# One block of a transformer on one core: the heads of an attention pair side by side in the matrix engine, and the gates' blocks between the pairs

## The chip, the cores and the metric

The kernel runs on one core of a Trainium2 chip. Five engines work there, each on a queue of its own that it takes in order: TensorE (PE, matmuls and transposes into the PSUM memory), VectorE (DVE), ScalarE (ACT), GpSimd (POOL) and SyncE (SP, which issues the loads). The metric is the device time of one execution in microseconds (us); lower is better.

## What is computed

The reference is two transformer blocks on 256 tokens of 1024 channels, in float32. The change is in the first half of the first block: a normalisation, one large projection, two attentions of 8 heads with 64 channels each, and a gated sum.

```python
h = rmsnorm(x, norm1_g)
qa, ka, va, qb, kb, vb, ga, gb = split(h @ w_in)
ya = neighbourhood_attention(qa, ka, va, rpb)        # scores + bias, window mask, softmax, @ va
qh = axial_rope(rmsnorm(qb, gqa_q_norm_g))           # rotation by row and column of the grid
kh = axial_rope(rmsnorm(kb, gqa_k_norm_g))
yb = gqa_attention(qh, kh, vb)                       # 8 query heads on 2 key/value heads
merged = sigmoid(ga) * (ya @ w_proj_a) + sigmoid(gb) * (yb @ w_proj_b)
x = x + merged @ w_out
```

Behind it come a layer of 16384 small experts (peer), and a second block with two recurrent mixers and a mixture of experts; the change leaves all of that as it is.

## The kernel before

A float32 product is done as three products of rounded parts. `split` (L65) makes the parts: ACT copies a value in rounded form (`whi`, L66), and DVE, or POOL where `eng` says so, subtracts that from the value (`wlo`, L67). `mm3` (L78) issues the three matmuls. `load_w` (L70) loads one block of weights, 128 partitions by 1024 values (512 KB), into a buffer `raw` and splits it. There are 4 `raw` buffers and 2 pairs of `whi` and `wlo`.

`block1_mix` (L143) is the first half of the first block. The normalised tokens lie transposed in `hT`. Then, in the order of the source:

- `qk_block` (L174): 8 blocks of 24 matmuls of 256 columns, queries and keys of the neighbourhood attention. In between the bias window and the mask are loaded, and POOL adds the mask to all of the bias at once (L246).
- `moving` (L179): 4 blocks of 12 matmuls of 512 columns for the values `va` (L256).
- four calls of `attention` (L197), one for each pair of heads.
- `moving` for the queries (4 blocks, `pq`) and for keys and values (2 blocks of 24 matmuls of 256 columns, `pkv`) of the second attention; then the rotation chain (L266 to L309) for both tiles of 128 tokens: squares, their sums, a reciprocal root by Newton steps (`rstd`, L92), products with the gains and the rotation's tables, all on DVE, then transposes `pqT` and `pkT` on PE and copies of them to `qT` and `kT`.
- four more calls of `attention`.
- 16 gate blocks (L316): `stationary` (L168), 24 matmuls of 256 columns each into a tile `pg`, copied by ACT into `sg`. The first 8 have their `wlo` made by POOL. At the end ACT takes four sigmoids of 4 blocks each (L321).

One call of `attention` does two heads `j`, whose queries and keys lie in partitions 0 to 63 and 64 to 127. Per head: scores `pS` (two matmuls of 64 rows, L204); in the neighbourhood attention DVE scales them and adds the bias (L211); DVE takes the negated maximum `mx`; ACT takes the exponentials with their sums (L220); DVE multiplies by the reciprocal sums (L224); PE transposes (`pT`, L228), and ACT copies the result (`PT`, L230). Then four matmuls `pY` (L235) multiply with the values of both heads, for each `j` all 128 columns of which only its own 64 are used, and `split` writes the halves of `yT`.

PSUM buffers come by tag: "mm" (4, projections and gates), "att" (2, `pS` and `pY`), "tr" (2, transposes). A scheduler that runs when the program is built sets the order of the instructions in each engine's queue: by order of the source, as far as it holds operands ready and buffers free; SP's order up to L251 is that of the source. What it fixes is final: on the chip each engine takes its queue in order.

Behind this part come the projections `pp` (L326 on), 8 blocks of 24 matmuls, which need the sigmoids and both `yT`.

## Time and profile before

| what | value |
|---|---|
| median of 3 runs | 1756.07 us (1755.73 to 1756.47) |
| the profiled execution, its own time | 1763.74 us |
| its span in the profile | 1761.9 us |
| PE busy | 1660.2 us, 94% of the span |
| DVE busy | 1133.1 us, 64% |
| ACT busy | 750.5 us, 43% |
| POOL busy | 190.5 us, 11% |
| the chain that ended last | PE 67%, DVE 18%, DMA 7%, issue 4%, ACT 3% |

Busy time is a share of the whole span; a stage has its own limit, and what an engine waits for is read from the timeline of that stage. In a timeline a row has the start, the duration, the engine, the line of the kernel, the operation and its tiles, and at the end, in brackets, how long the engine had been idle and who ended the wait. Float32 matmuls of this kernel count two records each, those of rounded parts one. PEclk is the clock that PE was granted, as a share of 2.4 GHz.

### The profile page before, as it was taken

The numbers are of one execution on the slowest core, as the hardware profiler recorded it, in microseconds if no ns is written. First come the engines' busy times: TensorE is split into PE (matmuls) and PEld (weight loads), VectorE is DVE, ScalarE is ACT, GpSimd is POOL, SyncE is SP. The second block draws the span as 40 slices with busy tenths as digits, with TensorE's granted clock in tenths as the row PEclk, the third lists the DMA queues.
The fourth block names the chain that finished last, engine by engine and source line by source line (L and its number), as shares of the span: only waits on it lengthen the run. The fifth ranks groups of instructions, "written<-read, shape, count | busy, mean of one in ns | idle before, by whom it ended". The sixth has DMA issues, their size and how long they took to land.

```text
span 1761.9 us, 29814 instructions
## 1 busy us (share of the span) xinstructions
PE 1660.2 (94%) x11419; PEld 1307.8 (74%) x11419; DVE 1133.1 (64%) x2214; ACT 750.5 (43%) x1224; POOL 190.5 (11%) x95
## 2 busy tenths in 40 slices
PE   6989999899989999999999997987989999999996
PEld 6778888899989999777788776977875444444443
DVE  5675779995989999877777767688673111111112
ACT  3547544444544444444444455655552222222222
POOL 1030001222111222000000003023020000000000
PEclk9999999999999999999999999998999999999999
DMA  6423654556545555587888754532067799999993
GB/s 232 131 84 109 214 163 158 160 158 192 155 126 162 169 171 177 172 283 265 308 283 295 261 165 144 181 118 72 13 238 282 266 392 409 409 402 409 409 409 132
DMA packets 108118, 390.91 MB, mean 222 GB/s; under 512 B 12656, under 2 KB 12944, under 8 KB 107840
## 3 DMA queue, kind: packets, MB, share of 16 engines
q1 hardware_dynamic: 106128, 384.58, 62.7%
q0 software_dynamic: 976, 2.82, 0.5%
q8 instruction: 91, 1.49, 0.3%
q10 hardware_dynamic: 864, 1.53, 0.3%
q14 instruction: 59, 0.48, 0.1%
HBM read 386.79 MB, written 2.10 MB: 221 GB/s over the span
## 4 chain that ended last, share of the span: by engine, by line
PE 67%; DVE 18%; DMA 7%; issue 4%; ACT 3%; POOL 0%; SPq 0%; DVEq 0%; ACTq 0%
PE pgu L1559 11%; PE acc L686 10%; PE py L1578 6%; PE pu L80 5%; PE pu L81 5%; PE pu L82 5%; DVE wlo L67 5%; DMA raw<-in_w_ada 4%; PE pga L1743 3%; PE py L1840 3%; PE pg L632 2%; ACT whi L66 2%; PE pmv L81 1%; PE pmv L82 1%; PE pmv L80 1%
## 5 line engine op out<-in xcount | busy, mean ns | idle before, releaser
L66 ACT ACTIVATE whi<-raw 128x1024 fp32r<-128x1024 f32 x366 | 384.5, 1054 | 307.7 <-PE pu L81 136.7
L67 DVE TENSOR_TENSOR wlo<-raw,whi 128x1024 fp32r<-128x1024 f32 x310 | 383.4, 1239 | 83.1 <-ACT whi L66 82.0
L82 PE MATMUL pu<-pxT,wlo 128*128 128x256 f32 x1024 | 289.7, 283 | 9.2 <-DVE wlo L67 6.7
L80 PE MATMUL pu<-pxT,whi 128*128 128x256 f32 x1024 | 292.3, 285 | 0.8 <-ACT whi L66 0.8
L81 PE MATMUL pu<-pxT,whi 128*128 128x256 f32 x1024 | 288.9, 282 | 0.0
L686 PE MATMUL acc<-whi,hh 128*128 128x512 f32 x1008 | 280.7, 396 | 8.5 <-ACT hh L66 5.8
L686 PEld LDWEIGHTS acc<-whi,hh 128*128 128x128 f32 x1008 | 189.1, 189 | 53.9 <-ACT hh L66 6.8
L67 POOL TENSOR_TENSOR wlo<-raw,whi 128x1024 fp32r<-128x1024 f32 x56 | 149.6, 2675 | 661.9 <-ACT whi L66 607.2
L82 PEld LDWEIGHTS pu<-pxT,wlo 128*128 128x128 f32 x1024 | 195.3, 191 | 11.1 <-DVE wlo L67 8.1
L80 PEld LDWEIGHTS pu<-pxT,whi 128*128 128x128 f32 x1024 | 195.4, 191 | 1.0 <-ACT whi L66 1.0
L81 PEld LDWEIGHTS pu<-pxT,whi 128*128 128x128 f32 x1024 | 195.4, 191 | 0.0
L1559 PE MATMUL pgu<-raw,xg 128*32 128x512 f32 (+2 forms) x1012 | 193.8, 597 | 0.0
L686 PE MATMUL acc<-wlo,hh 128*128 128x512 f32 x504 | 157.5, 393 | 2.8 <-DVE wlo L67 2.8
L66 ACT ACTIVATE hh<-H 128x256 fp32r<-128x256 f32 x126 | 52.6, 417 | 174.6 <-PE acc L686 169.9
L1559 PEld LDWEIGHTS pgu<-raw,xg 128*32 128x32 f32 (+2 forms) x1012 | 55.6, 124 | 92.3 <-issue 82.1
L686 PEld LDWEIGHTS acc<-wlo,hh 128*128 128x128 f32 x504 | 95.0, 189 | 24.3 <-DVE wlo L67 4.2
L67 DVE TENSOR_TENSOR yl<-py,yh 128x512 fp32r<-128x512 f32 x52 | 36.0, 691 | 110.7 <-ACT yh L66 110.6
L1578 PE MATMUL py<-raw,th 128*32 128x512 f32 (+2 forms) x504 | 99.9, 599 | 0.5 <-ACT th L1572 0.5
L1564 DVE SCALAR_TENSOR_TENSOR hh<-hh,sv,pgu 128x256 f32<-128x256 f32 x26 | 12.4, 478 | 124.5 <-ACT hh L1563 124.5
L771 DVE SCALAR_TENSOR_TENSOR ada<-raw,cs,ada 128x1024 f32<-128x1024 f32 x48 | 61.5, 1282 | 40.6 <-DMA raw<-in_w_ada 40.6
L1746 ACT ACTIVATE xg<-pga 128x256 f32<-128x256 f32 x104 | 40.0, 384 | 111.6 <-PE pga L1743 107.6
L1743 PEld LDWEIGHTS pga<-S,hs 128*128 128x128 f32 x416 | 54.5, 188 | 36.8 <-issue 36.1
(567 smaller groups left out, 2919.5 us busy)
## 6 DMA issues: line engine op xcount, KB each, us to landing
raw<-in_w_gu SPq DMA_DIRECT2D x186, 512.0 KB, 9.6
raw<-in_peer_u SPq DMA_DIRECT2D x128, 512.0 KB, 3.6
raw<-in_peer_v SPq DMA_DIRECT2D x128, 512.0 KB, 4.5
raw<-in_w_dn SPq DMA_DIRECT2D x90, 512.0 KB, 10.1
raw<-in_w_ada SPq DMA_DIRECT2D x48, 512.0 KB, 4.8
raw<-in_w_in_a SPq DMA_DIRECT2D x24, 512.0 KB, 3.6
raw<-in_w2a SPq DMA_DIRECT2D x17, 512.0 KB, 4.4
raw<-in_w_out SPq DMA_DIRECT2D x16, 512.0 KB, 3.6
```

The source lines that it names most:

```text
L66: e.nc.scalar.activation(hi, src, AF.Copy)
L67: (eng or e.nc.vector).tensor_sub(lo, src, hi.bitcast(F32))
L80: nc.tensor.matmul(out, lh, rh, start=first, stop=False)
L81: nc.tensor.matmul(out, lh, rl, start=False, stop=False)
L82: nc.tensor.matmul(out, ll, rh, start=False, stop=last)
L686: nc.tensor.matmul(acc[tt][n], h[l][:, s], w[r][:, n * 512:(n + 1) * 512], start=j == order[0] and i == 0, stop=j == order[-1] and i == 2)
L771: nc.vector.scalar_tensor_tensor(mod[n], w, cs[:, c:c + 1], mod[n], op0=OP.mult, op1=OP.add)
L1559: nc.tensor.matmul(pg[t], xx[:, c, t], ws[i][:, k * 512:(k + 1) * 512], start=c == 0, stop=c == NC8 - 1)
L1578: nc.tensor.matmul(py[q][t], th[:, k, t], w[i][:, q * 512:(q + 1) * 512], start=k == 0, stop=last and k == 1)
L1743: nc.tensor.matmul(p[:, :n].rearrange("p u n -> p (u n)"), hs[i][:, tt, q * P:(q + 1) * P], S[:, tt, :n].rearrange("p u n -> p (u n)"), st ...
L1746: nc.scalar.activation(xg[:, q, :n], p[:, :n], AF.Copy)
L1840: nc.tensor.matmul(acc[tt][n], St[:, tt * P:(tt + 1) * P], y[:, n * 512:(n + 1) * 512], start=first and v == 0 and w == 0, stop=v == len(u ...
```

## The change

It does five things, all in `block1_mix`.

- `attention` issues the scores of both heads first, one matmul of each head in turn, and then the softmax of the one and of the other. `pY` has four matmuls of 64 columns each, head 0 into partitions 0 to 63 and head 1 into 64 to 127 of one tile, in turn; the tile has the tag "mm" now, not "att". One `split` of 128 partitions follows in place of two of 64.
- `moving` for the second attention and the rotation chain stand ahead of the first `attention`.
- Two gate blocks follow each call of `attention`, in place of 16 behind the last.
- All `wlo` of the gates are made by DVE. The mask is added by DVE too, in four parts of 768 columns.
- The blocks of `w_in` are loaded by `wide_load` (L1407), a helper of the later layers, with 4 pairs of `whi` and `wlo`: the two old ones and two more in the pool `b1`. It takes the places of a list in turn:

```python
def load(src, whole=False, eng=None):
    raw.append(raw.pop(0))
    pool, bufs, tag = raw[-1]
    t = pool.tile([P, 1024], F32, tag=tag, name=uid(e, "raw"), bufs=bufs) if bufs else pool
    e.nc.sync.dma_start(t, src)
...
    parts.append(parts.pop(0))
    pool, bufs = parts[-1]
    hi, lo = (pool.tile([P, 1024], F32R, tag=g, name=uid(e, g), bufs=bufs) for g in ("whi", "wlo"))
    split(e, hi, lo, t, eng)
    return hi, lo
```

```diff
--- before.py
+++ after.py
@@ -164,9 +164,10 @@
 
 
     qkT = pool.tile([P, 8, T], F32, name="qkT")
+    load = wide_load(e, [(e.stage, e.raw_bufs)], [(e.stage, e.w_bufs), (pool, 2)])
 
     def stationary(blk, out, eng=None):
-        wh, wl = load_w(e, a["w_in_a"][blk], eng=eng)
+        wh, wl = load(a["w_in_a"][blk], eng=eng)
         wh, wl = (w.rearrange("p (c n) -> p c n", c=NC8) for w in (wh, wl))
         for c in range(NC8):
             mm3(e, out, wh[:, c], wl[:, c], hT[0][:, c], hT[1][:, c], c == 0, c == NC8 - 1)
@@ -180,7 +181,7 @@
 
         pt = [ps.tile([P, 512], F32, tag="mm", name=uid(e, "pmv"), bufs=e.mm_bufs) for _ in range(2)]
         for i, b in enumerate(blks):
-            wh, wl = load_w(e, a["w_in_b"][b])
+            wh, wl = load(a["w_in_b"][b])
             wh, wl = (w.rearrange("p (c n) -> p c n", c=per) for w in (wh, wl))
             for k in range(per):
                 c = i * per + k
@@ -196,12 +197,14 @@
 
     def attention(pair, q_of, k_of, v_of, bias_of, dst):
 
+
+        heads = [slice(j * 64, (j + 1) * 64) for j in range(2)]
+        pSs = [ps.tile([P, 2, T], F32, tag="att", name=uid(e, "pS"), bufs=e.att_bufs) for _ in heads]
+        for i, tt in enumerate((1, 0)):
+            for s, pS in zip(heads, pSs):
+                nc.tensor.matmul(pS[:, i], q_of(pair)[s, tt * P:(tt + 1) * P], k_of(pair)[s], start=True, stop=True)
         PT = []
-        for j in range(2):
-            s = slice(j * 64, (j + 1) * 64)
-            pS = ps.tile([P, 2, T], F32, tag="att", name=uid(e, "pS"), bufs=e.att_bufs)
-            for i, tt in enumerate((1, 0)):
-                nc.tensor.matmul(pS[:, i], q_of(pair)[s, tt * P:(tt + 1) * P], k_of(pair)[s], start=True, stop=True)
+        for j, pS in enumerate(pSs):
             S = wk.tile([P, 2, T], F32, tag="S", name=uid(e, "S"), bufs=2)
             mx = wk.tile([P, 2], F32, tag="mx", name=uid(e, "mx"), bufs=3)
             sm = wk.tile([P, 2], F32, tag="sm", name=uid(e, "sm"), bufs=3)
@@ -229,13 +232,11 @@
             pt = wk.tile([P, 2, T], F32, tag="PT", name=uid(e, "PT"), bufs=4)
             nc.scalar.activation(pt, pT, AF.Copy)
             PT.append(pt)
-        pY = ps.tile([P, 2, T], F32, tag="att", name=uid(e, "pY"), bufs=e.att_bufs)
-        for j in range(2):
-            for kc in range(2):
-                nc.tensor.matmul(pY[:, j], v_of(pair, kc), PT[j][:, kc], start=kc == 0, stop=kc == 1)
-        for j in range(2):
-            s = slice(j * 64, (j + 1) * 64)
-            split(e, dst[0][s, pair], dst[1][s, pair], pY[s, j])
+        pY = ps.tile([P, 512], F32, tag="mm", name=uid(e, "pY"), bufs=e.mm_bufs)[:, :T]
+        for kc in range(2):
+            for s, pt in zip(heads, PT):
+                nc.tensor.matmul(pY[s], v_of(pair, kc)[:, s], pt[:, kc], start=kc == 0, stop=kc == 1)
+        split(e, dst[0][:, pair], dst[1][:, pair], pY)
 
     for b in (0, 4, 1, 5):
         qk_block(b)
@@ -243,8 +244,6 @@
     nc.sync.dma_start(bias.rearrange("p a b c -> p (a b c)"), a["na_win"])
     mask = pool.tile([P, 64], F32, name="mask")
     nc.sync.dma_start(mask, a["na_mask"])
-    nc.gpsimd.tensor_tensor(bias.rearrange("p a b c -> p (a b) c"), bias.rearrange("p a b c -> p (a b) c"),
-                            mask[:, None, :].to_broadcast([P, 48, 64]), op=OP.add)
     rope = pool.tile([P, 2, 2, 64], F32, name="rope")
     nc.sync.dma_start(rope.rearrange("p a b c -> p (a b c)"), a["rope"])
     gqk = [row(e, pool, a["gqa_q_norm_g"], 64, "gq", eng=nc.sync), row(e, pool, a["gqa_k_norm_g"], 64, "gk", eng=nc.sync)]
@@ -254,11 +253,6 @@
         qk_block(b)
     for tt, p in enumerate(moving(range(0, 4), 512, 2)):
         nc.vector.tensor_copy(va[:, tt], p)
-    bv = bias.rearrange("p h v c -> p h (v c)")
-    for pair in range(4):
-        attention(pair, lambda q: qkT[:, q], lambda q: qkT[:, 4 + q],
-                  lambda q, kc: va[:, kc, q * P:(q + 1) * P], lambda h: bv[:, h], yT[0])
-
 
     pq = moving(range(4, 8), 512, 2)
     pkv = moving(range(8, 10), 256, 4)
@@ -307,16 +301,32 @@
         for k in range(2):
             nc.tensor.transpose(p[:, k], kf[:, k * P:(k + 1) * P], e.ident)
         nc.vector.tensor_copy(kT[:, :, tt * P:(tt + 1) * P], p[:, :2])
+
+    sg = keep.tile([P, 16, T], F32, name="sg")
+
+    def gate(b):
+        p = ps.tile([P, 512], F32, tag="mm", name=uid(e, "pg"), bufs=e.mm_bufs)
+        stationary(8 + b, p[:, :T])
+        nc.scalar.activation(sg[:, b], p[:, :T], AF.Copy)
+
+    bv = bias.rearrange("p h v c -> p h (v c)")
+
+    def masked(h):
+        if h % 2 == 0:
+            v = bias[:, h:h + 2].rearrange("p a b c -> p (a b) c")
+            nc.vector.tensor_tensor(v, v, mask[:, None, :].to_broadcast([P, 12, 64]), op=OP.add)
+        return bv[:, h]
+
+    for pair in range(4):
+        attention(pair, lambda q: qkT[:, q], lambda q: qkT[:, 4 + q],
+                  lambda q, kc: va[:, kc, q * P:(q + 1) * P], masked, yT[0])
+        for b in (2 * pair, 2 * pair + 1):
+            gate(b)
     for pair in range(4):
         attention(pair, lambda q: qT[:, q], lambda q: kT[:, q // 2],
                   lambda q, kc: vb[:, kc, q // 2].rearrange("p a b -> p (a b)"), None, yT[1])
-
-
-    sg = keep.tile([P, 16, T], F32, name="sg")
-    for b in range(16):
-        p = ps.tile([P, 512], F32, tag="mm", name=uid(e, "pg"), bufs=e.mm_bufs)
-        stationary(8 + b, p[:, :T], nc.gpsimd if b < 8 else None)
-        nc.scalar.activation(sg[:, b], p[:, :T], AF.Copy)
+        for b in (8 + 2 * pair, 9 + 2 * pair):
+            gate(b)
     for b in (0, 8, 4, 12):
         nc.scalar.activation(sg[:, b:b + 4], sg[:, b:b + 4], AF.Sigmoid)
     warm(e, AF.Sqrt, sg[:, 15, 0:1])
```

Three places show how the instructions move.

The first is PE's queue in the second attention, before: the transposes of the first pair (`pT`, `S`) stand among the matmuls of a gate block (`pg`).

```order
L82 MATMUL pg_1304<-hT_97,wlo_1308 128x256
L80 MATMUL pg_1304<-hT_97,whi_1307 128x256
L228 MATMUL pT_928<-ident,S_918 128x128
L81 MATMUL pg_1304<-hT_98,whi_1307 128x256
L228 MATMUL pT_928<-ident,S_918 128x128 x3
L82 MATMUL pg_1304<-hT_97,wlo_1308 128x256
L80 MATMUL pg_1304<-hT_97,whi_1307 128x256
L81 MATMUL pg_1304<-hT_98,whi_1307 128x256
L228 MATMUL pT_948<-ident,S_938 128x128
L82 MATMUL pg_1304<-hT_97,wlo_1308 128x256
L228 MATMUL pT_948<-ident,S_938 128x128 x3
```

Before, a matmul of the gate stands in front of each group of transposes. Now, at the same step of the first pair of all, right behind the matmuls of `pkv` and the scores of pair 0:

```order
L205 MATMUL pS_825<-qkT 128x256 x2
L205 MATMUL pS_826<-qkT 128x256 x2
L298 MATMUL pqT_679<-ident,qk_636 128x128 x4
L302 MATMUL pkT_685<-ident,kd_675 128x128 x2
L298 MATMUL pqT_700<-ident,qk_644 128x128 x4
L302 MATMUL pkT_706<-ident,kd_696 128x128 x2
L231 MATMUL pT_729<-ident,S_717 128x128 x4
L231 MATMUL pT_747<-ident,S_736 128x128 x4
L238 MATMUL pY_754<-PT_734,va 64x256
L80 MATMUL pg_761<-hT_97,whi_764 128x256
```

The scores of pair 1 (825, 826), the transposes of the rotation and those of pair 0 stand together, with no gate matmul between; the first gate matmul (`pg_761`) stands behind the first matmul of `pY`.

The second is PE's queue at the end of gate blocks 2 and 3, where pair 2 (`pS_939`, `pS_940`) comes to its transposes (`S_945`, `S_964`); the first row is the last matmul of gate block 3:

```order
L82 MATMUL pg_907<-hT_97,wlo_911 128x256
L205 MATMUL pS_939<-qkT 128x256
L205 MATMUL pS_940<-qkT 128x256
L205 MATMUL pS_1053<-qkT 128x256 x2
L205 MATMUL pS_1054<-qkT 128x256 x2
L231 MATMUL pT_957<-ident,S_945 128x128 x4
L231 MATMUL pT_975<-ident,S_964 128x128 x4
L238 MATMUL pY_982<-PT_962,va 64x256
L80 MATMUL pg_989<-hT_97,whi_992 128x256
```

The first halves of the scores of pair 2 stand ahead of gate block 2; the second halves, and the scores of pair 3 (1053, 1054), have moved behind gate block 3, directly ahead of the transposes.

The third is ACT's queue at the same place, from the split of gate block 7's weights to the copies of pair 2's transposes:

```order
L66 ACTIVATE whi_1138<-raw_1136 128x1024
L310 ACTIVATE sg<-pg_907 128x256
L331 ACT_TABLE_LOAD
L331 ACTIVATE sg<-sg 128x1024
L223 ACT_TABLE_LOAD
L223 ACTIVATE S_945,sm_947<-S_945,mx_946 128x256 x2
L223 ACTIVATE S_964,sm_966<-S_964,mx_965 128x256 x2
L233 ACTIVATE PT_962<-pT_957 128x512
L233 ACTIVATE PT_980<-pT_975 128x512
```

A sigmoid of gates 0 to 3 and two loads of function tables now stand between the copy of gate 3 and the exponentials of pair 2. On PE the places of pairs 4 and 7 read like that of pair 2; pair 4's exponentials have a sigmoid with two loads in front, pair 7's one load. In pair 5 both heads' scores stand behind gate block 9 in part. Pairs 1, 3 and 6 have all their scores ahead of two gate blocks. On SP the load of the second norm's gain (`g`) moves from place 17 to place 47, behind the fourth projection block. From the projections on, every engine has its instructions in the old order.

## Rows read from the trace of the kernel before

**Rows 1.** Timeline of PE, 53 to 54 and 172 to 173 us: start us, us, engine, line.
```profile
53.44 0.39 PE L82 MATMUL pmv<-whi,hT 128*128 128x512 f32 x1
54.12 0.39 PE L82 MATMUL pmv<-whi,hT 128*128 128x512 f32 x1
...
172.72 0.28 PE L80 MATMUL pg<-hT,whi 128*128 128x256 f32 x1
173.08 0.28 PE L80 MATMUL pp<-yTa,whi 128*128 128x256 f32 x1
```

**Rows 2.** Window: length; busy PE, PEld, DVE, ACT, POOL; PEclk; DMA; GB/s.
```profile
89.10:173.10 84.00, 75.12 (x511) 67.38 (x510) 54.84 (x106) 49.80 (x102) 17.30 (x7) 0.96 0.31 95
```

**Rows 3.** Timelines of POOL, DVE and PE around the mask's addition.
```profile
16.90 6.78 POOL L246 TENSOR_TENSOR bias<-bias,mask 128x3072 f32<-128x3072 f32 x1 [15.58 <-DMA mask<-in_na_mask]
...
19.38 5.38 DVE L67 TENSOR_TENSOR wlo<-raw,whi 128x1024 fp32r<-128x1024 f32 x1 [0.55 <-ACT whi L66]
...
24.82 0.38 PE L82 MATMUL pqk<-hT,wlo 128*128 128x256 f32 x1 [3.45 <-DVE wlo L67]
```

**Rows 4.** By line, 50 to 176 us: ns min/median/max, first and last start.
```profile
L109 DVE TENSOR_TENSOR gqr<-gqr,gqr x3: 178/178/178, 98.7 to 100.0; 128x20 f32<-128x20 f32 x3
L211 DVE SCALAR_TENSOR_TENSOR S<-pS,bias x16: 401/414/425, 55.7 to 90.3; 128x256 f32<-128x256 f32 x16
L213 DVE TENSOR_REDUCE mx<-S x8: 675/686/687, 57.5 to 91.4; 128x2 f32<-128x512 f32 x8
L224 DVE TENSOR_SCALAR S<-S,sm x32: 336/350/2190, 59.6 to 157.2; 128x256 f32<-128x256 f32 x32
L282 DVE TENSOR_TENSOR qk<-qk,gqr x2: 809/816/824, 100.4 to 103.3; 128x640 f32<-128x640 f32 x2
L283 DVE TENSOR_TENSOR qk<-qk,gq x2: 674/1776/2879, 102.5 to 107.0; 128x512 f32<-128x512 f32 x2
L291 DVE TENSOR_TENSOR ro<-qk,rope x4: 477/478/2133, 104.6 to 112.2; 128x320 f32<-128x320 f32 x4
L67 DVE TENSOR_TENSOR wlo<-raw,whi x17: 1214/1225/1227, 50.2 to 174.3; 128x1024 fp32r<-128x1024 f32 x17
```

**Rows 5.** Windows of PE: length, busy us, PEclk, DMA share, GB/s.
```profile
25.00:29.00 4.00, 4.00 (x24) 0.64 0.69 179
112.00:115.00 3.00, 3.00 (x15) 0.52 0.07 29
```

**Rows 6.** Timeline of ACT, a sigmoid between weight blocks.
```profile
113.80 1.06 ACT L66 ACTIVATE whi<-raw 128x1024 fp32r<-128x1024 f32 x1 [6.99 <-issue]
114.76 0.37 ACT L319 ACTIVATE sg<-pg 128x256 f32<-128x256 f32 x1
115.14 1.28 ACT L321 ACT_TABLE_LOAD   x1
116.44 1.06 ACT L321 ACTIVATE sg<-sg 128x1024 f32<-128x1024 f32 x1
```

**Rows 7.** Timeline of PE, the turned queries behind two waits.
```profile
111.98 1.09 PE L304 MATMUL pqT<-ident,qk 128*128 128x128 f32 x4 [2.93 <-DVE qk L299]
...
118.34 0.63 PE L304 MATMUL pqT<-ident,qk 128*128 128x128 f32 x4 [1.21 <-DVE qk L299]
```

**Rows 8.** Timelines of PE and ACT, first pair of the second attention.
```profile
120.18 1.14 PE L204 MATMUL pS<-kT,qT 64*128 64x256 f32 x8
...
123.62 0.48 ACT L220 ACTIVATE S<-pS,mx 128x256 f32<-128x256 f32 x1
...
126.32 0.27 PE L228 MATMUL pT<-ident,S 128*128 128x128 f32 x1
...
126.64 1.11 ACT L230 ACTIVATE PT<-pT 128x512 f32<-128x512 f32 x2
```

**Rows 9.** Timeline of PE, pY of a pair and one head's scores.
```profile
62.44 1.89 PE L235 MATMUL pY<-PT,va 128*128 128x256 f32 x8
64.26 1.13 PE L204 MATMUL pS<-qkT 64*128 64x256 f32 x4
```

## Prediction

> **What bounds the kernel now.** The change touches the first 185 of 1762 us only; behind the gates every engine's instructions stand in the order that they had, so the question is by how much the end of the gates moves. In the timeline of TensorE (PE) I set three marks: 54.3, the end of the last matmul of the neighbourhood values; 89.1, the first gate matmul; 173.1, where the first projection matmul follows the last gate matmul without a pause [rows 1]. A table by windows then shows that PE is idle for only 8.9 of the 84.0 us between the last two, at a mean granted clock of 0.96 [rows 2]. So PE is the bound, and its idle time is small because matmuls that nobody waits for (gates) stand between the steps of the softmax. Ahead of 54.3 there is one hole: GpSimd (POOL) adds the mask to the bias for 6.78 us, a VectorE (DVE) subtraction that takes 1.2 elsewhere takes 5.38 beside it, and PE stands for 3.45 [rows 3, 4].
>
> **Part by part.** The durations are those of the profiled execution (span 1761.9, time 1763.74). The median of the runs, 1756.07, lies 7.7 below its time; I add the difference that I work out to the median, unscaled.
>
> *Up to the end of the values.* The mask goes to DVE, in four additions of 768 columns. An operation of 640 columns takes 0.82 [rows 4]; by its columns that makes 0.97 each, 3.9 us in all, while DVE would otherwise stand in the long subtraction. With four pairs of weight buffers the first four blocks are split ahead, and this is the cover; if it fails, PE waits for at most one addition. The 3.45 go. So does the slow clock behind them: 0.64 over 25 to 29 us is 1.4 us of PE lost [rows 5]. The values end at 54.3 - 4.9 = 49.4. Now all four of the second attention's weight blocks and its two key and value blocks follow at once: 48 matmuls of 512 columns, one each 0.227, and 48 of 256, one each 0.12 (in both pairs of rows three matmuls lie between the starts [rows 1]), 16.6 us: 66.0.
>
> *The rotation chain, and pair 0.* This is the first large term. Before, gate matmuls and three pairs ran beside the rotation; now the order shows nothing on PE between the scores of pairs 0 and 1 and the turned queries. The new tag explains it: pY takes a buffer of "mm", the gates' own tag, so the gates' first matmul comes behind the first matmul of pY. PE therefore waits for DVE. Up to the first transposes DVE has, in its queue: seven operations of 640 columns, two of 512, three of 320, four of 128, thirteen small ones of the root, and among them the softmax of pair 0 (four additions of the bias, two maxima, two reciprocals, three scalings) and one wlo. An operation that follows another without a wait starts a little before that one ends (on ACT 1.06 behind 113.80, and the next at 114.76 [rows 6]); for DVE I take 0.08 off each row, and count the dependent small ones in full [rows 4]: 5.1 + 1.2 + 1.2 + 0.8 (128 columns, by the longer ones, 0.28 each) + 2.3 + 1.3 + 1.2 + 0.4 + 0.8 + 1.15, and 1.1 for the copy at the start (0.4, about ScalarE's 0.37 for 256 columns [rows 6]) and the last operation in full (0.7): 16.5. Second token tile: one of 320, one scaling, one of 640, the copies of the first tile's transposes, two of 128, one of 512 make 3.4 more: 19.9. Its transposes (0.65 [rows 7]), two copies (0.67 and 0.35, by their columns) that free the buffers that pair 0's transposes take, then transposes 0.7, copy 0.6, half of pY 0.6: 23.5. The first gate matmul comes at 66.0 + 23.5 = 89.5, 0.4 later than before, with pairs 1 to 7 still to do where four and a half were left.
>
> *The gates with seven pairs.* 16 x 24 matmuls at 0.12 make 46.1. What a pair adds depends on where its scores stand.
>
> Pairs 1, 3 and 6 have their softmax done while the gates run. After the last gate matmul the ScalarE (ACT) queue holds a whi (0.96) and a copy to sg (0.38) [rows 6], then two PT copies (1.11 [rows 8]), then half of pY (0.6): 3.2 with the gaps, 9.6 for three.
>
> Pairs 2 and 4 have half of their scores behind the gates. ACT then does whi, sg, a table load, a sigmoid (from 113.80 to the sigmoid's end near 117.4, 3.6 us [rows 6]) and a second load (1.28) before the exponentials begin at 5.0, though the maxima are there at about 2. From the first exponential to the second head's transposes took 2.7, a copy 0.6 [rows 8]; four transposes take 0.65 [rows 7], half of pY 0.6: 9.6 each, 19.2.
>
> Pair 7 has a load but no sigmoid in front. Half of the scores 0.6 [rows 8], two maxima of 0.69 [rows 4] and a scaling make 2.2, then 4.6 as above: 6.8. Pair 5 needs no load, but a wlo (1.15) and the first head's scaling stand in front of the second head's maximum, and its PT copy stands behind exponentials of pair 6: 7.9, of which six gate matmuls fill 0.7: 7.2.
>
> Together 9.6 + 19.2 + 6.8 + 7.2 = 42.8, less 0.8 for seven gate matmuls in the holes: 88.1 with the gates.
>
> *The clock.* After PE had waited for the rotation, the granted clock was 0.52 over 112 to 115, 1.4 us lost [rows 5]: four transposes took 1.09 there, behind a wait of 2.93, and 0.63 behind one of 1.21 [rows 7]. The holes behind the rotation and in pairs 2, 4 and 7 are longer than 2.9: 4 x 1.4 = 5.6. Bounds: none (0), or all eight pairs (11.2).
>
> *The sum.* 89.5 + 88.1 + 5.6 = 183.2 against 173.1: 10.1 us later, and 1756.07 + 10.1 = 1766.2.
>
> *Edits that I cost at nothing.* Eight wlo go from POOL to DVE (1.2 each [rows 4]): 9.8 us more on DVE, in the gates' shade, except where named above. One split of 128 partitions replaces two of 64 for yT; that is off PE's path. The load of the second norm's gain, a 512 KB row repeated over the partitions, moves in SP's queue from place 17 to 47, behind the fourth projection block; four more projection loads queue behind it, the first of them for the fifth block, 11 us behind the gates' end (4 x 24 matmuls). It is itself wanted only behind the projections; without that cover it costs one landing.
>
> *Both heads at a time.* For the scores the rows show it already: both heads of a pair took 1.14 [rows 8], one head alone 1.13 [rows 9]. So what is new is that all eight pairs get it. For pY no row shows heads in separate columns. The bounds for its four matmuls are half of the 1.89 that they take now [rows 9], 0.95, and all of it; I take 1.14, the scores' value, since two 64-wide pieces of the array ran side by side there. Half of it stands on the path; all of 1.89 would add 0.38 per pair, 3.0. The Trainium skill, "TensorEngine Tiling (Array Packing)", Key Properties, says that tiles load weights and multiply independently, which gives 1766.2; if columns do not follow that, the sum is 1769.2.
>
> A table load takes 1.28 in this trace [rows 6], and five stand on the path (two each in pairs 2 and 4, one in pair 7). The Trainium skill, "ScalarE: Activation LUTs", Terms, gives some 2.7 us for one. By that price the sum would be 7.1 higher, an estimate of 1773.3; the measured duration decides.
>
> **The rivals.**
>
> *Longer still.* The heads' columns take turns (3.0) and the clock falls in all eight pairs (5.6 more): 1774.8. For it: the trace has no column pieces, and both restarts [rows 5] ran slow. Against it: pairs 1, 3 and 6 leave PE idle for about 1 us at a time, and the wait of 1.21 did not slow it [rows 7]. The Trainium skill, "TensorE: Matmul & The Clock Gate", Part 3, The mechanism, says that a weight load overlaps running matmuls only when its row group differs; two column pieces share their rows, so by it they would partly take turns. No run here shows that.
>
> *No measurable change.* The clock holds through the holes (5.6), pY takes 0.95 (0.8), and the root's small operations hide their latency among the softmax ones (1.2): 7.6 less, 1758.6. For it: DVE does interleave two chains there. Against it: both long waits shown were followed by the slow clock [rows 5].
>
> *Faster.* The softmax of the next pair is done when the 48 gate matmuls of the pair before end, in pairs 2, 4, 5 and 7 too. Then each costs 3.2, which saves 20.4, and three restarts go, 4.2: 1741.6. It decides at the place of the second half of the scores: if they do not in fact wait for the gates. For it: 48 matmuls last 5.8 us and a softmax from scores to transposes took 6.1 [rows 8]; and PE does lose work: 12 heads stood alone (6 x 1.1), and pY gives 8 x 0.75, 12.6 us. Against it: in the order that second half stands behind the gates, and an engine takes its queue in order.
>
> **How the numbers follow.** My forecast, 1760 to 1773: 0.62. Longer still: 0.15. No measurable change: 0.14. Faster: 0.09, in which I also put that I misread the queues. A measurement of this kernel tells 0.2% (3.5 us) from no change, so 1752.6 to 1759.6 is "the same". Slower 0.62 + 0.15 = 0.77, same 0.14, faster 0.09. The range 1756 to 1776 takes in the forecast, the longer case at its price and the upper half of "no change".
>
> **What would show it.** The first gate matmul at about 89 to 91 us, the first projection matmul at 180 to 188 instead of 173. PE idle for some 18 us between scores of pair 1 and pY of pair 0, waiting for DVE's rotation; holes of 5 to 7 us behind gates 3, 7 and 13, with a table load, a sigmoid and a table load on ACT in the first two; the granted clock near 0.5 behind each. The 3.45 us hole at 21 us gone. pY's matmuls of a pair in about 1.1 us. From the projections on, the same durations. I am wrong if the gates end before 173, or if the holes lie elsewhere, for instance in DVE's wlo.

## The result, and the profile of the changed kernel

| | before | changed |
|---|---|---|
| median of the runs | 1755.9 (1753.47 to 1756.47) | 1778.55 (1774.02 to 1787.93) |
| ratio to before, 95% interval | | 1.0139 [1.0095, 1.0182] |
| span of the profiled execution | 1761.9 | 1778.7 |
| first gate matmul | 89.1 | 89.2 |
| first projection matmul | 173.1 | 193.3 |

The change made the kernel slower by 22.65 us. I had forecast slower by 10.1, with 1776 as the upper end of the range: the direction was right, the size was not. In the trace the first projection matmul comes 20.2 us later; the table of windows, read stage by stage, tells where. Up to the first gate nothing is lost. This is the end of the gates in the changed kernel, on TensorE (PE), beside [rows 1]:

```profile
193.21 0.28 PE L82 MATMUL pg<-hT,wlo 128*128 128x256 f32 x1
193.32 0.28 PE L80 MATMUL pp<-yTa,whi 128*128 128x256 f32 x1
```

The windows (length; busy PE, PEld, DVE, ACT, POOL; granted clock; DMA share; GB/s) of the wait for the rotation, of the gates with seven pairs, and of four stretches in them:

```profile
66.00:89.20 23.20, 10.29 (x38) 6.53 (x38) 20.92 (x56) 6.34 (x17) 0.00 (x0) 0.60 0.15 46
89.20:193.30 104.10, 87.37 (x551) 68.92 (x551) 41.82 (x94) 53.51 (x115) 0.00 (x0) 0.88 0.22 66
111.50:118.50 7.00, 5.19 (x18) 3.15 (x19) 3.67 (x11) 3.25 (x10) 0.00 (x0) 0.51 0.20 70
139.00:145.00 6.00, 5.23 (x17) 3.27 (x19) 1.56 (x6) 2.82 (x10) 0.00 (x0) 0.50 0.13 55
156.00:163.00 7.00, 7.00 (x24) 4.37 (x24) 2.83 (x10) 3.20 (x11) 0.00 (x0) 0.52 0.25 75
183.00:187.50 4.50, 3.89 (x17) 2.38 (x17) 1.47 (x6) 1.98 (x6) 0.00 (x0) 0.62 0.00 0
```

Between 89.2 and 193.3 PE is idle for 16.7 of 104.1 us, where [rows 2] have 8.9 of 84.0, and part of its busy time is slow work: beside the wait for the rotation there are four stretches of 4.5 to 7 us in which the clock is mostly at 1.2 of 2.4 GHz (0.50 to 0.62 in the rows). The list of PE's waits from 14 to 215 us (us in total, times, longest) names what it waited for, the three largest first; the 3.45 us for a wlo in [rows 3] are gone from it:

```profile
PE pqT L298 <- DVE qk L293: 9.5, 2, 7.7
PE pT L231 <- DVE S L227: 7.4, 2, 4.5
PE pS L205 <- ACT S L223: 5.4, 1, 5.4
```

The order shows why PE has nothing else to do. The matmuls of the sixteen gate blocks used to stand between the steps of the softmaxes, as fillers. Now a pair's gates stand behind its pY, and so behind its whole softmax. How much a pair adds I read "from gate to gate": from the start of the last gate matmul ahead of its steps to the start of the first one behind them in an unbroken row. Pair 5 in PE's timeline:

```profile
151.60 0.28 PE L82 MATMUL pg<-hT,wlo 128*128 128x256 f32 x1
...
151.81 1.13 PE L205 MATMUL pS<-kT,qT 64*128 64x256 f32 x6
155.10 1.28 PE L205 MATMUL pS<-kT,qT 64*128 64x256 f32 x4 [2.15 <-DVE wlo L67]
...
157.35 2.07 PE L205 MATMUL pS<-kT,qT 64*128 64x256 f32 x4
159.35 0.47 PE L231 MATMUL pT<-ident,S 128*128 128x128 f32 x1
...
163.88 0.39 PE L80 MATMUL pg<-hT,whi 128*128 128x256 f32 x1
```

Here pair 6's scores (155.10 and 157.35) stand ahead of the second head's transposes (159.35 and later), and the first of them wait 2.15 until the first head's exponentials, which end at 155.04, have freed a buffer. (The row names a wlo that ended at 155.06; it is a gate's, and the scores don't use it.) Four score records without a partner in other rows take as long as eight with one (1.13 at full clock, [rows 8, 9]), and at half clock 2.07. From gate to gate it is 163.88 - 151.60 = 12.28. Pair 2, in the same view:

```profile
106.28 0.28 PE L82 MATMUL pg<-hT,wlo 128*128 128x256 f32 x1
...
113.31 2.07 PE L231 MATMUL pT<-ident,S 128*128 128x128 f32 x8 [2.89 <-DVE S L227]
115.31 1.12 PE L238 MATMUL pY<-PT,va 128*64 128x256 f32 x2
...
118.83 0.39 PE L80 MATMUL pg<-hT,whi 128*128 128x256 f32 x1
```

Here eight transposes take 2.07 behind a wait of 2.89, against 1.03 in the pairs that the gates cover. Of those, pair 1:

```profile
97.11 1.03 PE L231 MATMUL pT<-ident,S 128*128 128x128 f32 x8
...
99.06 1.56 PE L238 MATMUL pY<-PT,va 128*64 128x256 f32 x8 [0.28 <-ACT PT L233]
100.56 0.39 PE L80 MATMUL pg<-hT,whi 128*128 128x256 f32 x1
```

Its last gate matmul starts at 96.99, so it adds 3.57. And pair 7, on DVE, ACT and PE:

```profile
179.12 1.29 DVE L219 TENSOR_REDUCE mx<-pS 128x2 f32<-128x512 f32 x2 [4.64 <-PE pS L205]
...
180.56 1.28 ACT L223 ACT_TABLE_LOAD   x1 [1.69 <-DVE mx L220]
181.86 0.47 ACT L223 ACTIVATE S<-pS,mx 128x256 f32<-128x256 f32 x1
...
183.61 2.00 PE L231 MATMUL pT<-ident,S 128*128 128x128 f32 x8 [4.52 <-DVE S L227]
...
185.54 2.00 PE L238 MATMUL pY<-PT,vb 128*64 128x256 f32 x8
```

### The profile page after: what moved, and what is told of

It is laid out like the page before. It is cut to its first block, busy times and chain, and to the rows that moved or that the text cites. A ratio compares the mean times of both kernels' runs of the same rounds, so it can differ in the third digit from the quotient of the medians.

```text
span 1778.7 us, 29811 instructions
## 1 busy us (share of the span) xinstructions
PE 1662.2 (93%) x11419; PEld 1302.3 (73%) x11419; DVE 1123.2 (63%) x2218; ACT 749.5 (42%) x1218; POOL 166.3 (9%) x86
## 4 chain that ended last, share of the span: by engine, by line
PE 67%; DVE 17%; DMA 8%; issue 4%; ACT 3%; POOL 0%; DVEq 0%; SPq 0%; ACTq 0%
PE pgu L1569 10%; PE acc L696 7%; DMA raw<-in_w_ada 6%; PE py L1588 6%; PE pu L80 5%; PE pu L82 5%; PE pu L81 5%; DVE wlo L67 5%; PE pga L1753 3%; PE py L1850 3%; PE pg L642 2%; ACT whi L66 1%; PE pmv L82 1%; PE pmv L80 1%; PE pmv L81 1%
## 5 line engine op out<-in xcount | busy, mean ns | idle before, releaser
L66 ACT ACTIVATE whi<-raw 128x1024 fp32r<-128x1024 f32 x366 | 384.4, 1054 | 313.4 <-PE pu L81 138.5
L67 DVE TENSOR_TENSOR wlo<-raw,whi 128x1024 fp32r<-128x1024 f32 x318 | 389.0, 1226 | 99.6 <-ACT whi L66 99.0
L67 POOL TENSOR_TENSOR wlo<-raw,whi 128x1024 fp32r<-128x1024 f32 x48 | 131.9, 2750 | 570.8 <-ACT whi L66 569.4
## 6 DMA issues: line engine op xcount, KB each, us to landing
raw<-in_w_dn SPq DMA_DIRECT2D x90, 512.0 KB, 10.1
```

The lines of the kernel that those rows point to most:

```text
L66: e.nc.scalar.activation(hi, src, AF.Copy)
L67: (eng or e.nc.vector).tensor_sub(lo, src, hi.bitcast(F32))
```

## The experiments

Theory A: one line, the tag of pY, ties each pair's gates behind its pY; the holes that this opens and the slow clock behind them are the loss, and the other parts of the change gain. Against it stood: the column pieces, VectorE's (DVE's) extra work and the moved rotation cost by themselves (B, C), and, for the size, the clock against the queues. "The mark" below is the first projection matmul of a profiled execution.

| run | median us | ratio to before, 95% interval | the mark |
|---|---|---|---|
| e1 pY in "att" | 1750.66 | 0.9952 [0.9929, 0.9974] | 150.8, but see there |
| e2 before + packed heads | 1755.89 | 0.9983 [0.9961, 1.0005] | 169.0 |
| e3 e2 + mask on DVE, buffers | 1750.85 | 0.9952 [0.9935, 0.9969] | 165.2 |
| e4 changed, sigmoids last | 1773.37 | 1.0080 [1.0056, 1.0105] | 186.0 |
| e5 changed, bank claimed early | 1740.17 | 0.9901 [0.9877, 0.9926] | 152.7 |
| e6 changed, pairs 2 and 7 filled | 1778.19 | 1.0107 [1.0083, 1.0130] | 190.7 |
| e7 changed, rotation back | 1783.00 | 1.0143 [1.0122, 1.0164] | 198.5 |
| e8 before + tag of pY | 1782.61 | 1.0129 [1.0105, 1.0153] | 195.5 |
| e9 e6 + pair 5 filled | 1774.47 | 1.0084 [1.0056, 1.0112] | 187.4 |
| e10 changed, load early | 1783.85 | 1.0138 [1.0090, 1.0185] | 194.7 |
| e11 changed, load early, again | 1776.89 | 1.0111 [1.0095, 1.0128] | 193.1 |
| e12 e5 with the old pY | 1740.86 | 0.9910 [0.9893, 0.9926] | 155.8 |

The kernel before ran beside each of them, with medians of 1756.48 to 1762.20, so the ratios, not the medians, compare them with each other.

### e8: the tag alone, in the kernel before

```diff
-pY = ps.tile([P, 2, T], F32, tag="att", ..., bufs=e.att_bufs)
+pY = ps.tile([P, 512], F32, tag="mm", ..., bufs=e.mm_bufs).rearrange("p (a b) -> p a b", a=2)
```

> The kernel before with one edit: pY takes a buffer of "mm". Theory A: this line alone takes the cover away. In the order no gate stands between the pairs any more, all 384 gate matmuls come in one row at the end, and the rotation and eight softmaxes are bare; TensorE's idle time ahead of the last gate goes from 9 to 30 us or more, and the time to 1778 (1768 to 1790), with nothing else of the change in it. Rival: the tag is harmless without the gates' new places: 1756.

Measured: 1782.61, and the whole loss is there with nothing else of the change. All 384 gate matmuls stand in one row at the end. First the largest of PE's waits up to the gates' end, then the window of [rows 2], here up to 195.4, in which PE is idle for 20.8 us at a clock of 0.87:

```profile
PE pqT L304 <- DVE qk L299: 14.7, 2, 12.9
```

```profile
89.10:195.40 106.30, 85.46 (x564) 74.91 (x563) 47.08 (x99) 46.92 (x95) 19.22 (x8) 0.87 0.33 100
```

What follows: the tag is enough to cause the loss. A buffer of a tag is given out in the order of the source; a gate's tile comes behind pY's in that order, and pY's is first written when the softmax is done.

### e5: the tie undone, and nothing else

```diff
+bank = ps.tile([P, 512], F32, tag="mm", ..., bufs=e.mm_bufs)
+nc.tensor.matmul(bank[:, T:], hT[0][:, 0, :P], hT[0][:, 1], start=True, stop=True)
 PT = []
...
-pY = ps.tile([P, 512], F32, tag="mm", ..., bufs=e.mm_bufs)[:, :T]
+pY = bank[:, :T]
```

> The changed kernel, pY still in the gates' tag "mm", but one matmul (0.12 us) writes the unused half of pY's bank before the softmax of its pair, eight in all; nothing reads it. The bank is thereby taken early, and the gates that follow in the source need not wait for pY. Theory A (it is the order in which the tag gives out its buffers that ties the gates behind pY): the gates move into the softmaxes and beside the rotation, the last gate ends before 170, the time is 1750 (1744 to 1757), as with e1. Rival (e1 gained because pY left the gates four buffers): gates still stand idle for want of buffers, 1765 or more.

Measured: 1740.17, below its range, 38 us less than the changed kernel (42 by the ratios) and 1% less than before. The windows (columns as above), with the wait for the rotation in the first:

```profile
66.00:89.20 23.20, 21.15 (x166) 19.27 (x166) 23.20 (x58) 15.00 (x29) 0.00 (x0) 1.00 0.31 89
89.20:152.70 63.50, 62.33 (x432) 49.17 (x431) 37.90 (x92) 44.14 (x104) 0.00 (x0) 1.00 0.31 94
```

PE is busy for 83.48 of 86.7 us at full clock. So the tie is necessary for the loss too, and the rival of too few buffers falls: pY still takes one of the gates' four. The other parts of the change together are worth 1% to the kernel before; the tie took that and 1.4% more.

### e1: the other way out, pY back in "att"

```diff
-pY = ps.tile([P, 512], F32, tag="mm", ..., bufs=e.mm_bufs)[:, :T]
+pY = ps.tile([P, 2, T], F32, tag="att", ..., bufs=e.att_bufs)[:, 0]
```

> The changed kernel with one edit: pY takes a buffer of the tag "att" again instead of one of the gates' tag "mm". Theory A (the tag ties each pair's gates behind its pY; everything else in the change is harmless or useful): gates run beside the rotation and inside each softmax, so TensorE's idle time between 66 and the end of the gates falls from about 30 us to under 10, the slow-clock stretches go, the last gate matmul comes near 160 instead of 193, and the time is about 1742 (1735 to 1750), below the kernel before. Rival B (the edits themselves cost: column pieces, wlo on DVE, the rotation moved ahead): DVE or the rotation bounds the stretch, the time stays at 1765 or more.

Measured: 1750.66; B falls. It is 8.7 us above my figure, just outside the range, and slower than e5. The trace shows the gates running too far ahead: pY now competes with the scores for two "att" buffers, the gates are used up while pairs 6 and 7 are still under way, and those run bare between the projections. By tile, these matmuls of the projections start from 150.8 to 183.9, a stretch that took 20 us before:

```profile
L80 PE MATMUL pp<-yTa,whi x32: 280/283/416, 150.8 to 183.9; 128*128 128x256 f32 x32
```

### e2, e3 and e12: what the edits are worth

e2 puts the new attention (pY in "att") into the kernel before, e3 adds the mask's four additions on DVE and the wider buffers, e12 puts the old pY into e5:

```diff
-pY = bank[:, :T]
-for kc in range(2):
-    for s, pt in zip(heads, PT):
-        nc.tensor.matmul(pY[s], v_of(pair, kc)[:, s], pt[:, kc], start=kc == 0, stop=kc == 1)
-split(e, dst[0][:, pair], dst[1][:, pair], pY)
+pY = bank.rearrange("p (a b) -> p a b", a=2)
+for j in range(2):
+    for kc in range(2):
+        nc.tensor.matmul(pY[:, j], v_of(pair, kc), PT[j][:, kc], start=kc == 0, stop=kc == 1)
+for j, s in enumerate(heads):
+    split(e, dst[0][s, pair], dst[1][s, pair], pY[s, j])
```

> The kernel before with one edit: both heads of a pair in rows (scores) and columns (pY) of their own, one split of 128 partitions for yT; gates, mask, weight buffers and rotation as before. Theory A: pure gain of TensorE time, 12 heads that stood alone give about 0.55 each and pY 0.33 per pair (1.89 to 1.56), 9.2 us less TensorE work, so 1747 (1744 to 1751). If column pieces cost in themselves (rival B): pY takes 1.9 or more and the time is 1753 to 1760.

> e2 plus the mask on VectorE in four additions and four pairs of weight buffers, so everything of the change but the gates' place, pY's tag, the rotation's place and GpSimd's eight wlo. Theory A: the stall of 3.45 at 21 us and its slow clock of 1.4 go besides, 4.9 below e2: 1742 (1738 to 1746), the fastest of the four. If the mask only moves the wait (rival): no faster than e2.

> e5 with pY as in the kernel before: four matmuls with all 128 columns of the values for each pair, and two splits of 64 partitions; scores, mask, rotation, gates as in e5. There TensorE is busy for nearly the whole stretch, so what the column pieces save of TensorE's time shows in full. By e2's busy times (17.9 us of pY against 13.1, eight pairs) the last gate ends 4.8 later than in e5, at 157.5, and the time is 1745 (1741 to 1749). If the pieces take turns in the array and only their number differs: 1740, as e5.

Measured: 1755.89, 1750.85 and 1740.86. Windows of 50 to 200 us for one tile (columns as above), first the scores and then pY. The kernel before:

```profile
50.00:200.00 150.00, 16.61 (x64) 9.20 (x64) 11.69 (x24) 8.35 (x32) 0.98 0.37 116
...
50.00:200.00 150.00, 17.91 (x64) 11.53 (x64) 6.74 (x16) 6.06 (x16) 0.98 0.37 116
```

e2:

```profile
50.00:200.00 150.00, 16.61 (x64) 9.17 (x64) 11.54 (x24) 8.14 (x32) 0.98 0.40 121
...
50.00:200.00 150.00, 13.10 (x64) 5.43 (x64) 3.36 (x8) 3.05 (x8) 0.98 0.40 121
```

e5:

```profile
50.00:200.00 150.00, 11.85 (x64) 6.63 (x64) 11.42 (x24) 7.85 (x32) 1.00 0.45 141
...
50.00:200.00 150.00, 15.37 (x72) 6.71 (x72) 3.39 (x8) 3.07 (x8) 1.00 0.45 141
```

e12:

```profile
50.00:200.00 150.00, 9.35 (x64) 5.44 (x64) 11.56 (x24) 7.77 (x32) 1.00 0.45 135
...
50.00:200.00 150.00, 18.70 (x72) 12.75 (x72) 6.74 (x16) 6.03 (x16) 1.00 0.45 135
```

The scores of a pair are cheaper only where both heads' matmuls stand side by side. In e2 the order still sets the heads apart in six of eight pairs, and the 16.61 us stay; in e12, where they stand together in all eight, it is 9.35. Column pieces save 4.8 of 17.9 us of pY in e2 and 3.3 of 18.7 in e12 (e5 and e12 have the eight claiming matmuls in their rows). They could save more: where both heads' operands are there, all eight records of a pair take 1.09, as in this pair of e5, against the 1.89 of [rows 9]:

```profile
121.39 1.09 PE L240 MATMUL pY<-PT,vb 128*64 128x256 f32 x8
```

Mostly the second head's copy PT comes later than the first's. The heads alternate in the queue, so the first head's first matmul then runs alone, and its second one stands behind the other head's first, which waits.

In e2 PE reaches the rotation sooner and waits there 6.2 instead of 4.1, so the mark moves by 4.1 and the time by less than its interval can tell from nothing: my 1747 was wrong by the scores. e3 is 5.0 below e2, near the 4.9 expected, but its own figure of 1742 (1738 to 1746) was missed, since e2 gained less. The intervals of the two ratios overlap, so the marks have to tell: the first matmul of the values starts at 38.9 instead of 43.4, and the mark comes 3.8 sooner. e12's time is that of e5 within the intervals; its mark is 3.1 later, less than the 4.8 expected, since its scores happen to stand together more often. In its list of PE's waits, PE waits 3.9 us for DVE's scalings where e5 waits 0.7; DVE has 16 subtractions for yT there, 6.74 us, instead of 8 (3.39): part of what the pieces give may be VectorE's time, which wasn't tested by itself.

### e6 and e9: the clock

```diff
+for _ in range({2: 24, 7: 24}.get(pair + (4 if bias_of is None else 0), 0)):
+    nc.tensor.matmul(last[0][:, T:], hT[0][:, 0, :P], hT[0][:, 1], start=True, stop=True)
 PT = []
```

e9 has {2: 24, 5: 16, 7: 24}; `last[0]` is the bank of the last gate.

> The changed kernel with 24 more matmuls of 256 columns (2.9 us at full clock) behind the second half of the scores in pairs 2 and 7, where TensorE stood idle; they write the unused half of the last gate's bank, and nothing reads them. The order is otherwise that of the changed kernel. Theory: the idle wait is what brings the slow clock, and the slow clock doubles the transposes and pY on the pair's own path: the granted clock behind these two pairs stays near 1.0, transposes take 1.03 instead of 2.0, pY 1.6 instead of 2.7, each pair is 2 us shorter, the last gate ends near 189 instead of 193, 1774.5 (1772 to 1777). If the clock is not set by the idle wait, or the pair's end by the other engines: 1778 or more.

> e6 with 16 such matmuls more (1.9 us) between the scores of pair 5 and those of pair 6, where TensorE stood for 2.15; the order is otherwise unchanged. Pair 5 is the term that the forecast missed most: 12.3 us from gate to gate in the changed kernel, 7.2 forecast without a slow clock. If the slow clock is its larger part, the clock stays near 1.0 there and the pair falls to 9.8 or less, the last gate ends near 188, and the time is 1773 (1770 to 1777). If the larger part is the queue (the second head's transposes stand behind the scores of pair 6, which wait for a buffer that the first head's exponentials free): 11 or more from gate to gate even at full clock, the last gate near 190, no change against e6 (1778).

Measured: e6 1778.19, outside its range, a time that can't be told from the changed kernel's; e9 1774.47, as expected. The intervals of the two overlap; the marks, 190.7 and 187.4 against 193.3, and the traces tell more. Pair 2 of e6 on PE, with the granted clock of the stretch behind its filler:

```profile
112.84 0.72 PE L235 MATMUL pT<-ident,S 128*128 128x128 f32 x4 [1.25 <-DVE S L231]
...
114.47 0.65 PE L242 MATMUL pY<-PT,va 128*64 128x256 f32 x2
...
115.60 1.08 PE L242 MATMUL pY<-PT,va 128*64 128x256 f32 x6
116.61 0.39 PE L80 MATMUL pg<-hT,whi 128*128 128x256 f32 x1
```

```profile
113.00:118.00 5.00, 4.73 (x30) 3.23 (x30) 3.65 (x10) 2.57 (x8) 0.00 (x0) 1.00 0.00 0
```

The clock stays at 1.00 and four transposes take 0.72; from gate to gate pair 2 falls from 12.55 to 10.80. Pair 7 hardly gains (9.29 to 9.13, now with three gate matmuls in it, without which it would be 8.8): there the scalings on DVE and the copies on ScalarE (ACT) between the steps take the time that the clock gives back. Pair 5 of e9:

```profile
152.65 1.13 PE L207 MATMUL pS<-kT,qT 64*128 64x256 f32 x4
...
154.29 1.13 PE L207 MATMUL pS<-kT,qT 64*128 64x256 f32 x4
...
158.43 0.39 PE L80 MATMUL pg<-hT,whi 128*128 128x256 f32 x1
```

The second piece of pair 6's scores takes 1.13 instead of 2.07, and pair 5 is 9.47 instead of 12.28: 2.8 us of it were the slow clock. With all three filled the mark is 187.4 against 193.3: 1.75, 0.5 (with the three gate matmuls) and 2.8 come from the three pairs, 0.9 from the rest of pair 0, which the edit doesn't touch: there the clock came back sooner. Pair 4, the same in kind as pair 2, wasn't filled.

### e4, e10 and e11: ACT's tables

```diff
 # e4
+zero = keep.tile([P, 1], F32, name="zero")
+nc.scalar.activation(zero, sg[:, 15, 0:1], AF.Copy, scale=0.0)
...
+    nc.scalar.activation(sg[:, b:b + 4], sg[:, b:b + 4], AF.Sigmoid, bias=zero)
 # e10; e11 reads sg[:, 13, 0:1] instead
+if bias_of is None and pair == 3:
+    warm(e, AF.Exp, pSs[0][:, 0, 0:1])
```

> The changed kernel with the four sigmoids held behind the last gate (their bias is a zero that is written from the last gate's output); TensorE's order is unchanged. The forecast's price: two table loads and a sigmoid stand before the exponentials of pairs 2 and 4, a load before pair 7. Without them the holes of pairs 2 and 4 shrink by 2.8 each and that of pair 7 by 1.3: about 7 us, 1771 (1768 to 1774). If the holes are set by TensorE's slow clock and VectorE alone: no change, 1778.

> The changed kernel with one more exponential of a single column in pair 7, which reads the scores and not their maximum, so that ScalarE loads its table while VectorE takes the maxima; TensorE's order is unchanged. In the trace of the changed kernel that load began only when the scaled maximum was there (180.56), and its 1.28 lay on the path; the forecast had let it run beside the maxima. Expected: the load begins near 179.2, pair 7 takes 8.0 instead of 9.3 from gate to gate, the last gate ends 1.3 earlier (192.0), which the time (1777, 1774 to 1780) hardly shows. If the load waits all the same: 9.3.

> e10 again with another operand: the one-column exponential reads the last gate's copy in sg instead of the scores, since in e10 VectorE's maximum waited for ScalarE's reading of the same scores (181.07 behind 180.78), so that the load stayed on the path. Expected: the load begins near 179 right behind that copy, the maxima start 0.1 behind the scores as in the changed kernel, and pair 7 takes 8.0 instead of 9.3 from gate to gate; the last gate 1.3 earlier, the time 1777 (1773 to 1781). If the load was no part of pair 7's path: 9.3 again.

Measured: e4 1773.37, within its range, and the mark 7.3 sooner, but not for the reason that I gave: the hit is luck. Pairs 2 and 4 take 11.98 and 12.33 from gate to gate, only 0.6 and 0.4 less (with six and three more gate matmuls in them), not 2.8 each. TensorE's order did shift, against what I wrote: pair 5's scores now stand ahead of pair 4's transposes, and pair 7's ahead of pair 6's. Pair 5 takes 3.6 instead of 12.3, pair 7 3.3 instead of 9.3, and pair 6 13.5 instead of 3.6. So e4 doesn't price the tables. e10 missed (1783.85, above its range, and 10.0 from gate to gate): ACT loads at 179.49, but DVE's maximum now comes behind ACT's reading of the same scores, and the load stays on the path:

```profile
179.49 1.28 ACT L116 ACT_TABLE_LOAD   x1
...
181.07 1.29 DVE L221 TENSOR_REDUCE mx<-pS 128x2 f32<-128x512 f32 x2 [6.00 <-ACT junk L116]
```

e11 puts the load beside the maxima, and the transposes start 3.94 behind the start of the scores (181.82 - 177.88) instead of 5.22, 1.28 sooner, so the load was on the path. The time, 1776.89, is in its range, yet pair 7 takes 9.9 from gate to gate, not the 8.0 expected and no less than 9.3. The slow clock begins sooner here and lasts longer: by the rows below, from 181.8 to 188 PE is at half clock for about 5.6 us, in the changed kernel, by its row of 183 to 187.5, for about 3.4. The timeline of ACT and PE, and the clock:

```profile
178.38 1.28 ACT L116 ACT_TABLE_LOAD   x1
...
181.82 2.00 PE L233 MATMUL pT<-ident,S 128*128 128x128 f32 x8 [3.24 <-DVE S L229]
...
185.74 1.90 PE L240 MATMUL pY<-PT,vb 128*64 128x256 f32 x6
```

```profile
181.80:184.00 2.20, 2.18 (x9) 1.63 (x10) 0.92 (x4) 0.94 (x4) 0.00 (x0) 0.50 0.00 0
184.00:186.00 2.00, 2.00 (x7) 1.02 (x8) 0.00 (x0) 0.45 (x1) 0.00 (x0) 0.50 0.00 0
186.00:188.00 2.00, 2.00 (x9) 0.93 (x8) 0.00 (x0) 0.33 (x1) 0.00 (x0) 0.64 0.00 0
```

### e7: the rotation

```diff
...
+for pair in range(4):
+    attention(pair, ..., masked, yT[0])
+    for b in (2 * pair, 2 * pair + 1):
+        gate(b)
 pq = moving(range(4, 8), 512, 2)
...
```

> The changed kernel with the second attention's projections and the rotation chain back behind the first four pairs (and their gates), pY still in "mm". Theory A: the place of the chain is not the cause; TensorE stands bare beside it at either place, and pair 0 loses its cover, so no gain: 1779 (1773 to 1786). Rival C (moving the chain ahead of the pairs opened the hole): 1765 or less.

Measured: 1783.00, inside its range; C falls, as long as pY stays in "mm". With the chain behind four pairs and their gates, PE waits for it for 14.6 us in two waits, against 9.5 in the changed kernel. Without fillers it is bare at either place.

## Why the prediction was wrong, step by step

**Up to the first gate: right in sum, in part by luck.** Forecast 66.0 for the end of the projections and 89.5 for the first gate matmul; the last projection matmul starts at 65.66, the first gate at 89.21. The stall of 3.45 went with its slow clock: the first matmul of the values starts 5.2 sooner than before (38.2 against 43.4), and 4.5 sooner in e3 than in e2, around the 4.9 forecast. In the rotation two errors cancel. The second tile's transposes start at 84.40, 1.5 ahead of the 85.9 of the sum; the steps from there to the first gate take 4.8 at half clock instead of 3.6.

**The order and its cause: right.** pY's tag ties the gates behind it; e8 and e5 show it both ways. The first hole lies where I put it, and the table loads and sigmoids stand on ACT ahead of the exponentials of pairs 2 and 4 as described.

**"The gates with seven pairs" and "The clock": too small by 10.4**, and this is the step that failed: 104.1 us from the first gate to the projections, forecast 93.7 (88.1 and 5.6). From gate to gate, with the six gate matmuls that I set off against pair 5 added back:

| pairs | forecast, clock included | measured | what the runs showed |
|---|---|---|---|
| rest of pair 0 | 1.4 | 2.2 | three of pY's four matmuls behind the first gate: 1.3 in e6 and e9; clock 0.9 |
| 1, 3, 6 | 3 x 3.2 = 9.6 | 3 x 3.57 = 10.7 | the same three matmuls behind the second copy |
| 2, 4 | 2 x (9.6 + 1.4) = 22.0 | 12.55 + 12.74 = 25.3 | chain 10.8 at full clock in pair 2 (e6); clock 1.75 |
| 5 | 7.2 + 0.7 = 7.9 | 12.3 | chain 9.5 at full clock (e9); clock 2.8 |
| 7 | 6.8 + 1.4 = 8.2 | 9.3 | chain 8.8 at full clock (e6); clock 0.5 |

Counting pair 4 like pair 2, which is an estimate, about 8.5 of the miss is there at full clock too, and about 2 is the clock's. Three terms of the chain were wrong, as the next paragraphs say, and the clock was left out of pair 5.

**"Half of pY (0.6)" is the term that was wrong in every pair.** The price of 1.14 for pY's matmuls was right: with both heads ready they take 1.09 (e5). What was wrong is how much of pY waits for the second head's copy. Since the heads alternate in the queue, it is three matmuls of four. In pair 1 the second copy ends at 99.49 in ACT's timeline, and the next gate starts at 100.56, 1.07 later; in e6's pairs 2 and 7 it is 1.43, since three gate matmuls end in between. In e6's pair 2 the two parts can be seen as 0.65 and 1.08. Over the eight pairs that makes about 5 us, by the same estimate. All of one head and then all of the other was not tried with column pieces.

The Trainium skill, "TensorEngine Tiling (Array Packing)", Key Properties, has tiles load weights and multiply independently; e5's 1.09 for eight records, beside 1.14 for the eight of the scores, agrees. The Trainium skill, "TensorE: Matmul & The Clock Gate", Part 3, The mechanism, has a weight load overlap running matmuls only when its row group differs; the two column pieces share their rows and still take the time of one, so here that rule is not borne out.

**Pair 5 is the largest miss of a single pair.** I booked no restart there, though PE has nothing to do until the first head's exponentials free a buffer, which is the hole of 2.15 us. And I overlooked that pair 6's scores, four records alone, stand in PE's queue ahead of its second transposes: 1.1 at full clock (e9), 2.0 at half.

**In pair 7 I let the table load run beside the maxima.** It began only with the scaled maximum (180.56), and its 1.28 came on top.

**The clock's 1.4 for a restart** lies between what it cost in pair 2 (1.75) and in pair 7 (0.5); pair 5's 2.8 was not booked at all. Counting pair 4 like pair 2, it is 7.7 in place of 5.6. The slow stretches of pairs 2 and 5 lasted some 7 us (0.51 and 0.52 in the rows), longer than the 3 to 4 in [rows 5]. And at half clock the work that runs here is not filler but the path itself: transposes, pY and, in pair 5, scores.

**The table load was 1.28** in each row, as booked. The Trainium skill, "ScalarE: Activation LUTs", Terms, gives 2.7; the sum by that price, 1773.3, lies nearer to the result, but no row of this case bears it out: the exponential starts at 181.86, right behind the load of 180.56.

**The rivals.** "Longer still", 1774.8, came nearest, by luck: the columns do not take turns (1.09 in e5), and the clock fell in pairs 0, 2, 4, 5 and 7, not in all. "Faster" held what the change has to give: 12.6 us of TensorE's work. PE's scores do fall by 7.3 (16.61 to 9.35 in e12, forecast 6.6) and pY by 3 to 5 (forecast 6.0); it only needs the gates as fillers, which e5 gives back. The remaining difference, 22.65 against the 20.2 of the mark, is within the scatter named below.

**What stays open.** Pair 4 at full clock wasn't tried; the order of pY's matmuls was read from the queue and not changed in a run; why pair 7 in e11 ends no sooner is read from the clock rows and wasn't tested further; e5 and e12 aren't told apart by time.

## What to carry to other kernels

A tag with several users is a queue: its buffers go out in source order, so a tile whose first writer is late blocks every later user of the tag. Before a tile changes its tag, look in the order at what now stands behind it; if the filler work does, take the buffer early (one small independent matmul per pair did, 38 us) or leave it where it was. And a hole on TensorE in a chain of short steps is to be priced as the wait and the slow clock behind it, on each step that the path still has, with whatever else stands in the queue between them. Where two heads alternate in one queue, the first head's second step stands behind the other head's first: ask whose operand comes last before half of the work is priced as done.

## What was not expected of the hardware

- **The rest of the program scatters by 12 us.** From the first matmul of the block's output projection on, PE's instructions stand in the same order in all these kernels but e1; in their thirteen profiled executions that part took from 1552.9 (e4) to 1565.3 us (before). It doesn't follow the edits, but the granted clock of that part goes with it: 0.98 in the seven executions of 1559.7 us and more, 0.99 in the six of 1557.2 and less; which causes which isn't shown. So single times differ by 0.5% and more (before: 1752.97 to 1767.32 over all its runs). A difference of a few us is read from marks in the traces, not from the times.
- **Column pieces of the array overlap as fully as row pieces, if both are ready**: eight records of pY take 1.09 in e5, where eight of the scores take 1.14. With the second head's operand late, as in the covered pairs, they take 1.56, against 1.89 in turn.
- **A shorter hole need not end sooner**: in e11 the transposes came 1.28 earlier and the pair's end did not, with the clock at 0.50 from 181.8 to 186.
